# First mixer of a two-layer decoder step: GELU and swish as one ScalarE instruction each, layer norm as two VectorE operations

## The chip, the cores and the metric

The kernel runs on one core of one Trainium2 chip. The metric is the device time of one execution in microseconds (us), and the median of the runs stands for a kernel. The engines are named as the profile names them: PE is TensorE (its matmuls; PEld is its weight load), DVE is VectorE, ACT is ScalarE, POOL is GpSimd, and SP is SyncE, whose queue issues the weight transfers.

## The reference, cut to what matters

The step serves 256 prompt positions and 64 sample positions (NT = 320 columns in all) with the same weights. The first layer has the mixer that the change touches; `u`, `v` and `gate` are three of the six column blocks of one input projection.

```python
def layer_norm(x, g, b):
    mu = jnp.mean(xf, axis=-1, keepdims=True)
    xc = xf - mu
    y = xc * lax.rsqrt(jnp.mean(xc * xc, axis=-1, keepdims=True) + EPS)
    return y * g + b

def sgu_mix(u, v, ln_g, ln_b, w_s, b_s):
    vn = layer_norm(v, ln_g, ln_b)
    ...
    mixed = jnp.einsum('gts,bnsgd->bntgd', w, vc) + b_s[...]
    return u * mixed.reshape(b, l, SGU_WIDTH), vc

def even_mixer(h, pos, s0, w_in, ln_g, ln_b, w_s, b_s, w_out):
    z = h @ w_in
    u, v, q, k, vr, gate = jnp.split(z, EVEN_SPLITS, axis=-1)
    a_out, v_rows = sgu_mix(jax.nn.gelu(u), jax.nn.gelu(v), ln_g, ln_b, w_s, b_s)
    ...
    b_out = o * jax.nn.silu(gate)
    y = jnp.concatenate([a_out, b_out], axis=-1) @ w_out
```

`jax.nn.gelu` is the tanh form. Behind the mixer come a cross attention and an MLP, then a second layer with windowed attention, a cross attention and an MLP; none of that is changed.

## The kernel before, in words

Every weight is split in two parts, `whi` (written by ACT as a rounding copy of the staged weight) and `wlo` (DVE: staged weight minus `whi`), and every projection is three matmuls for each pair of a weight tile and an activation tile (`whi` with the rounded activations, `whi` with their rest, `wlo` with the rounded ones). A weight piece of 1 MB comes in through SP into one of three `stage` buffers; it is split into two halves of 128x1024, and the split of the next piece is made while PE works on this one (`weights`, `split`). So PE can begin a group of 48 matmuls only when ACT and DVE have made that group's halves, and SP can issue a load only when the piece three places earlier has been consumed.

Projections come in two shapes. `gemm2` makes two chunks of features (128x320 each) in two PSUM banks called `mm`; with `serial` the first chunk is finished before the second is begun. `gemm_tok` makes tokens on partitions (128x512) for two prompt blocks and a folded sample block. Each group has an `evac` that takes the banks out. Small matmuls of the retention and the spatial mix use four banks called `at`; they stand in the PE queue at fixed places, by `hook`.

The mixer runs in this order: q and k (four `gemm2` groups), v of the gMLP (two `gemm_tok` blocks of two weight pieces, evacuated into `VA`, with `bn_stats` on each tile), v of the retention (two blocks, `VR`) with `layer_norm` hooked into the first of their pieces, u (four groups, evacuated into `AHh`/`ALl`, which the profile calls HH and HL), the first half of the output projection with the retention states of the samples beside it (`ret_cross`, `ret_upd`, each state written back by the POOL queue as `o_ret_s`), the gates (four groups into `BH`/`BL`, again HH and HL in the profile), and the second half of the output projection.

The scheduler of the framework sets the order on each engine from the program and its own estimates; each engine then runs its queue strictly in order. All compute instructions are recorded by one wrapper (`InOrder.call`), so they share line 64 (62 in the changed kernel) and are told apart by the names of their tiles: `t` are the 128x320 work tiles of an evacuation, `w` the 128x512 ones, `k` and `k8b` tiles of the retention.

GELU of u is written here as z = u/2 (the row `nm.RB` was halved by POOL beforehand), ACT Square, a DVE operation, ACT Tanh, a POOL product of z with the mixed values, and a DVE operation `(p + 1) * z`. GELU of v is the same with a copy out of PSUM in front. The swish is ACT Tanh of half the gate, the POOL product with the retention output, and the same DVE operation. `layer_norm` takes mean and scale off with one DVE operation for each of three tiles (128x1024 twice, 64x1024) and applies gain and bias with two POOL operations for each.

Of the kernel before, what the change touches and what calls it, by code (L numbers as in the profile page):

```python
# [12 lines left out]
AF = mybir.ActivationFunctionType  # L13
ALU = mybir.AluOpType
# [3 lines left out]
P = 128  # L18
NT = 320
# [3 lines left out]
GC = 0.7978845608028654  # L23
GA = 0.044715
# [51 lines left out]
def decoder_step(ctx: ExitStack, tc: tile.TileContext, d, plan):  # L76
# [9 lines left out]
    def sb(shape, tag, bufs=1, dt=F32):  # L86
        cnt[0] += 1
        return pool.tile(list(shape), dt, tag=tag, bufs=bufs, name=f"{tag}_{cnt[0]}")
# [551 lines left out]
    A.activation(warm, ones[:, 0:1], AF.Exp)  # L640
# [58 lines left out]
    def rs_apply():  # L699
        for c in (4, 5, 6, 7, 0, 1, 2, 3):  # L700
            (V if c % 4 == 3 else G).tensor_tensor(QK[:, c], QK[:, c], nm.RB, op=ALU.mult)
        G.tensor_scalar(nm.RB, nm.RB, 0.5, 0.0, op0=ALU.mult, op1=ALU.add)
# [74 lines left out]
    for blk in range(2):  # L777
        def evac(ps, blk=blk):
            for tb in range(3):
                w = P if tb < 2 else 64  # L780
                z = sb([P, 512], "w2", W2)
                if tb < 2:
                    A.activation(z, ps[tb], AF.Copy, scale=nm.rs[:, tb:tb + 1])
                else:
                    fs = fold_sample(ps[2], 512, False)
                    V.tensor_scalar(z[:64], fs, nm.rs[:64, 2:3], None, op0=ALU.mult)
                p = sb([P, 512], "w2", W2)
                A.activation(p[:w], z[:w], AF.Square)
                V.scalar_tensor_tensor(p[:w], p[:w], 1.0 / GA, z[:w], op0=ALU.add, op1=ALU.mult)
                A.activation(p[:w], p[:w], AF.Tanh, scale=GC * GA)  # L790
                o = VA[tb][:, blk * 512:(blk + 1) * 512]
                V.scalar_tensor_tensor(o, p[:w], 1.0, z[:w], op0=ALU.add, op1=ALU.mult)
                V.bn_stats(stats[:w, tb, blk], o)
        gemm_tok([("w_in", "tok", 1024 + blk * 512, kh) for kh in range(2)], nm.h, nm.l, XS, 512, evac)
# [5 lines left out]
    def layer_norm():  # L800
        for tb in range(3):
            w = P if tb < 2 else 64
            V.bn_aggr(ag[:w, tb], stats[:w, tb])
        V.tensor_scalar(lt, ag[:, :, 1], 0.25, EPS, op0=ALU.mult, op1=ALU.add)
        rsqrt_into(lr, lt, [P, 3])
        V.tensor_scalar(lr, lr, 0.5, None, op0=ALU.mult)
        for tb in range(3):
            w = P if tb < 2 else 64
            vt = VA[tb]
            V.tensor_scalar(vt, vt, ag[:w, tb, 0:1], lr[:w, tb:tb + 1], op0=ALU.subtract, op1=ALU.mult)  # L810
            G.tensor_tensor(vt, vt, lngb[:w, 0], op=ALU.mult)
            G.tensor_tensor(vt, vt, lngb[:w, 1], op=ALU.add)
        G.dma_start(d["sgu_v"], VA[2])
# [160 lines left out]
    for g in range(4):  # L974
        def evac(ps, i0=0, g=g):
            for i in range(len(ps)):
# [3 lines left out]
                p = sb([P, NT], "t1", 3)  # L980
                A.activation(p, z, AF.Square)
                V.scalar_tensor_tensor(p, p, 0.25 / GA, z, op0=ALU.add, op1=ALU.mult)
                A.activation(p, p, AF.Tanh, scale=8.0 * GC * GA)
# [11 lines left out]
                G.tensor_tensor(z, z, mix, op=ALU.mult)  # L995
                V.scalar_tensor_tensor(z, p, 1.0, z, op0=ALU.add, op1=ALU.mult)
# [8 lines left out]
    for g in range(4):  # L1005
        def evac(ps, i0=0, g=g):
            for i in range(len(ps)):
# [3 lines left out]
                p = sb([P, NT], "t1", 3)  # L1011
                A.activation(p, z, AF.Tanh)
                G.tensor_tensor(z, z, ON[0][:, c], op=ALU.mult)
                V.scalar_tensor_tensor(z, p, 1.0, z, op0=ALU.add, op1=ALU.mult)
# [599 lines left out]
```

## Time and profile before

| what | value |
|---|---|
| median of 3 runs | 1123.97 us (1122.43 to 1125.91) |
| the profiled execution's own time | 1124.34 us |
| its span, first to last instruction | 1122.6 us |
| mean granted TensorE clock of the span | 0.989 |
| busy: PE, PEld, DVE, ACT, POOL | 1086.4, 1021.9, 738.8, 524.2, 136.3 us |
| chain that ended last, by engine | PE 74%, DVE 13%, DMA 5%, ACT 4%, issue 2%, POOL 1% |

The busy times are those of one profiled execution. A matmul's record reaches into that of the next, so that a busy PE may still be late; how far apart matmuls start tells more. In the chain of work that ended last, time put down to DVE, ACT, POOL or a transfer is time in which the path to the end ran through them; it isn't all a hole of PE, since that path also runs through work that PE had just caught up with.

### The profile page before, as it was taken

What the parts mean: (1) busy time and instruction counts of PE and PEld (TensorE: products, weight loads), DVE (VectorE), ACT (ScalarE), POOL (GpSimd) and SP (SyncE); (2) the same over time, 40 slices, a digit from 0 to 9 for tenths busy, and PEclk for the clock granted to TensorE, in tenths of its full rate; (3) what the DMA queues carried; (4) which work ended last, traced back from release to release, by engine and by line L of the source; (5) the groups of instructions that cost most, each with busy time, mean ns of one, the idle gap of its engine ahead of it and who ended that gap; (6) DMA issues with size and microseconds to landing.
All of it is one profiled execution on the core that took longest, in us unless ns stands there. A gap on an engine that the chain in (4) does not pass through costs nothing.

```text
span 1122.6 us, 18500 instructions
## 1 busy us (share of the span) xinstructions
PE 1086.4 (97%) x7424; PEld 1021.9 (91%) x7424; DVE 738.8 (66%) x1447; ACT 524.2 (47%) x910; POOL 136.3 (12%) x131
## 2 busy tenths in 40 slices
PE   7998999999999999999999989999999999999996
PEld 7886979999987999999999988879968999999995
DVE  8999885776545575555556898956536855555543
ACT  6454641545325355444445557745323654343432
POOL 4506030123000010000001222002000200000001
PEclk9999999999999999999999989999999999999998
DMA  9432337744787644444444334547576444444421
GB/s 349 146 128 98 131 119 271 287 148 152 296 328 309 263 151 150 151 150 151 150 151 150 121 113 156 188 149 278 209 300 264 149 150 151 150 151 150 151 75 48
DMA packets 30982, 201.55 MB, mean 180 GB/s; under 512 B 3624, under 2 KB 4792, under 8 KB 7992
## 3 DMA queue, kind: packets, MB, share of 16 engines
q1 hardware_dynamic: 27584, 187.13, 45.8%
q0 software_dynamic: 2512, 11.54, 2.8%
q10 hardware_dynamic: 800, 1.70, 0.5%
q8 instruction: 58, 0.95, 0.3%
q14 instruction: 28, 0.23, 0.1%
HBM read 187.51 MB, written 12.85 MB: 178 GB/s over the span
## 4 chain that ended last, share of the span: by engine, by line
PE 74%; DVE 13%; DMA 5%; ACT 4%; issue 2%; POOL 1%; SPq 0%; ACTq 0%; DVEq 0%; POOLq 0%
PE mm L64 64%; PE at L64 10%; DVE wlo L64 5%; DMA stage<-ws 4%; DVE t L64 2%; ACT whi L64 2%; DVE w L64 1%; POOL t L64 1%; DVE XL L64 1%; ACT w L64 1%; ACT k L64 1%; DVE Z L64 0%; DVE k8b L64 0%; DVE nw_u L64 0%; DVE X L64 0%
## 5 line engine op out<-in xcount | busy, mean ns | idle before, releaser
L64 DVE TENSOR_TENSOR wlo<-stage,whi 128x1024 fp32r<-128x1024 f32 (+1 forms) x270 | 339.5, 1264 | 191.6 <-ACT whi L64 189.9
L64 ACT ACTIVATE whi<-stage 128x1024 fp32r<-128x1024 f32 (+1 forms) x270 | 280.2, 1050 | 363.5 <-PE mm L64 273.4
L64 PE MATMUL mm<-HH,whi 128*128 128x320 f32 (+1 forms) x960 | 294.4, 308 | 2.2 <-ACT HH L64 2.2
L64 PE MATMUL mm<-HL,whi 128*128 128x320 f32 (+1 forms) x960 | 293.8, 306 | 0.3 <-DVE HL L64 0.2
L64 PE MATMUL mm<-HH,wlo 128*128 128x320 f32 (+1 forms) x960 | 293.3, 306 | 0.0
L64 PE MATMUL mm<-XH,whi 128*128 128x320 f32 x912 | 286.9, 315 | 5.3 <-ACT whi L64 5.3
L64 PE MATMUL mm<-XH,wlo 128*128 128x320 f32 x912 | 283.9, 311 | 5.5 <-DVE wlo L64 5.3
L64 PE MATMUL mm<-XL,whi 128*128 128x320 f32 x912 | 283.4, 311 | 0.0
L64 PEld LDWEIGHTS mm<-HH,whi 128*128 128x128 f32 x960 | 180.7, 188 | 4.9 <-ACT HH L64 2.4
L64 PEld LDWEIGHTS mm<-HL,whi 128*128 128x128 f32 x960 | 181.0, 189 | 1.0 <-DVE HL L64 0.8
L64 PEld LDWEIGHTS mm<-HH,wlo 128*128 128x128 f32 x960 | 180.9, 188 | 0.1
L64 PEld LDWEIGHTS mm<-XH,whi 128*128 128x128 f32 x912 | 172.8, 189 | 6.9 <-ACT whi L64 5.3
L64 PEld LDWEIGHTS mm<-XH,wlo 128*128 128x128 f32 x912 | 172.6, 189 | 6.7 <-DVE wlo L64 6.7
L64 PEld LDWEIGHTS mm<-XL,whi 128*128 128x128 f32 x912 | 172.8, 189 | 0.7
L64 POOL TENSOR_TENSOR ssq<-ssq,sqt 128x320 f32<-128x320 f32 x39 | 41.6, 1068 | 609.0 <-ACT sqt L64 608.1
L64 DVE TENSOR_TENSOR X<-mm,X 128x320 f32<-128x320 f32 x112 | 51.7, 488 | 56.8 <-PE mm L64 56.6
L64 ACT ACTIVATE t<-t 128x320 f32<-128x320 f32 x88 | 38.0, 462 | 24.1 <-DVE t L64 24.1
L64 DVE SCALAR_TENSOR_TENSOR t<-mm,RB 128x320 f32<-128x320 f32 x64 | 30.1, 491 | 25.5 <-PE mm L64 22.6
L64 ACT ACTIVATE HH<-t 128x320 fp32r<-128x320 f32 x80 | 34.5, 462 | 21.6 <-DVE t L64 21.1
L64 DVE TENSOR_TENSOR HL<-t,HH 128x320 fp32r<-128x320 f32 x80 | 37.0, 491 | 9.9 <-ACT HH L64 9.3
L64 DVE SCALAR_TENSOR_TENSOR XL<-X,cv,XH 128x320 fp32r<-128x320 f32 x48 | 38.4, 822 | 4.7 <-ACT XH L64 4.7
L64 ACT ACTIVATE XH<-X,cv 128x320 fp32r<-128x320 f32 x48 | 26.3, 554 | 21.1 <-DVE X L64 19.3
(240 smaller groups left out, 1139.3 us busy)
## 6 DMA issues: line engine op xcount, KB each, us to landing
stage<-ws SPq DMA_DIRECT2D x162, 1024.0 KB, 4.8
o_ret_s<-stage POOLq DMA_DIRECT2D x8, 512.0 KB, 6.9
HH<-ws SPq DMA_DIRECT2D x4, 1024.0 KB, 6.8
HL<-ws SPq DMA_DIRECT2D x4, 1024.0 KB, 6.6
k8a<-ws SPq DMA_DIRECT2D x2, 1024.0 KB, 8.3
o_mem_k<-k8a POOLq DMA_DIRECT2D x2, 1024.0 KB, 8.2
o_mem_v<-k8b POOLq DMA_DIRECT2D x2, 1024.0 KB, 10.6
cst<-ce SPq DMA_DIRECT2D x1, 1296.0 KB, 10.3
```

Source lines behind the costliest of these rows:

```text
L64: r = f(*a, **k)
```

## The change

GELU becomes one ACT instruction (`Gelu_apprx_tanh`), for v read from the PSUM bank with the row scale as the instruction's scale, for u in place on the scaled tile. Swish becomes one ACT instruction (`Silu`) in place. The products with the mixed values and with the retention output move from POOL to DVE, and take the place of the DVE operations that closed the old forms. Layer norm becomes two DVE operations for each tile: (v - mean) * gain, and then * rstd + bias; its six POOL operations are gone, and so is POOL's halving of `nm.RB`.

```diff
-    A.activation(warm, ones[:, 0:1], AF.Exp)
+    A.activation(warm, ones[:, 0:1], AF.Gelu_apprx_tanh)
...
             (V if c % 4 == 3 else G).tensor_tensor(QK[:, c], QK[:, c], nm.RB, op=ALU.mult)
-        G.tensor_scalar(nm.RB, nm.RB, 0.5, 0.0, op0=ALU.mult, op1=ALU.add)
...
         def evac(ps, blk=blk):
             for tb in range(3):
                 w = P if tb < 2 else 64
-                z = sb([P, 512], "w2", W2)
+                o = VA[tb][:, blk * 512:(blk + 1) * 512]
                 if tb < 2:
-                    A.activation(z, ps[tb], AF.Copy, scale=nm.rs[:, tb:tb + 1])
+                    A.activation(o, ps[tb], AF.Gelu_apprx_tanh, scale=nm.rs[:, tb:tb + 1])
                 else:
                     fs = fold_sample(ps[2], 512, False)
-                    V.tensor_scalar(z[:64], fs, nm.rs[:64, 2:3], None, op0=ALU.mult)
-                p = sb([P, 512], "w2", W2)
-                A.activation(p[:w], z[:w], AF.Square)
-                V.scalar_tensor_tensor(p[:w], p[:w], 1.0 / GA, z[:w], op0=ALU.add, op1=ALU.mult)
-                A.activation(p[:w], p[:w], AF.Tanh, scale=GC * GA)
-                o = VA[tb][:, blk * 512:(blk + 1) * 512]
-                V.scalar_tensor_tensor(o, p[:w], 1.0, z[:w], op0=ALU.add, op1=ALU.mult)
+                    A.activation(o, fs, AF.Gelu_apprx_tanh, scale=nm.rs[:64, 2:3])
                 V.bn_stats(stats[:w, tb, blk], o)
...
-        V.tensor_scalar(lt, ag[:, :, 1], 0.25, EPS, op0=ALU.mult, op1=ALU.add)
+        V.tensor_scalar(lt, ag[:, :, 1], EPS, None, op0=ALU.add)
         rsqrt_into(lr, lt, [P, 3])
-        V.tensor_scalar(lr, lr, 0.5, None, op0=ALU.mult)
         for tb in range(3):
...
-            V.tensor_scalar(vt, vt, ag[:w, tb, 0:1], lr[:w, tb:tb + 1], op0=ALU.subtract, op1=ALU.mult)
-            G.tensor_tensor(vt, vt, lngb[:w, 0], op=ALU.mult)
-            G.tensor_tensor(vt, vt, lngb[:w, 1], op=ALU.add)
+            V.scalar_tensor_tensor(vt, vt, ag[:w, tb, 0:1], lngb[:w, 0], op0=ALU.subtract, op1=ALU.mult)
+            V.scalar_tensor_tensor(vt, vt, lr[:w, tb:tb + 1], lngb[:w, 1], op0=ALU.mult, op1=ALU.add)
         G.dma_start(d["sgu_v"], VA[2])
...
                 V.tensor_tensor(z, ps[i][:, :NT], nm.RB, op=ALU.mult)
-                p = sb([P, NT], "t1", 3)
-                A.activation(p, z, AF.Square)
-                V.scalar_tensor_tensor(p, p, 0.25 / GA, z, op0=ALU.add, op1=ALU.mult)
-                A.activation(p, p, AF.Tanh, scale=8.0 * GC * GA)
+                A.activation(z, z, AF.Gelu_apprx_tanh)
                 mp = bank("at")
...
-                G.tensor_tensor(z, z, mix, op=ALU.mult)
-                V.scalar_tensor_tensor(z, p, 1.0, z, op0=ALU.add, op1=ALU.mult)
+                V.tensor_tensor(z, z, mix, op=ALU.mult)
                 A.activation(AHh[:, c], z, AF.Copy)
...
                 V.tensor_tensor(z, ps[i][:, :NT], nm.RB, op=ALU.mult)
-                p = sb([P, NT], "t1", 3)
-                A.activation(p, z, AF.Tanh)
-                G.tensor_tensor(z, z, ON[0][:, c], op=ALU.mult)
-                V.scalar_tensor_tensor(z, p, 1.0, z, op0=ALU.add, op1=ALU.mult)
+                A.activation(z, z, AF.Silu)
+                V.tensor_tensor(z, z, ON[0][:, c], op=ALU.mult)
                 A.activation(BH[:, c], z, AF.Copy)
```

The queues of PE and SP hold the same instructions in the same order as before. DVE has 20 instructions fewer (14 of the GELU of v, 8 of the GELU of u, one of the scale, and three more for the layer norm), ACT 18 fewer and two table loads more, POOL 23 fewer. Behind the mixer the only difference is one of these table loads.

The DVE queue around the layer norm, before: `HH_478` and `k8b_480` are the v tiles, `e_ag` and `e_lr` the mean and the scale, `wlo_920` and `wlo_924` the split of the second piece of the second VR block, and `e_t` begins a norm of the retention.

```order
L64 TENSOR_SCALAR e_lr_778<-e_lr_778 128x3
L64 TENSOR_SCALAR HH_478<-HH_478,e_ag_775,e_lr_778 128x1024 x2
L64 TENSOR_SCALAR k8b_480<-k8b_480,e_ag_775,e_lr_778 64x1024
L64 TENSOR_TENSOR w_154_911<-at_781,w_153_909 64x512
L64 TENSOR_TENSOR wlo_920<-stage_917,whi_919 128x1024
L64 TENSOR_SCALAR k8b_480<-w_154_911,rs_333 64x512
L64 TENSOR_TENSOR wlo_924<-stage_917,whi_923 128x1024
L64 TENSOR_SCALAR e_t_946<-e_ss_942 128x2
```

The same place now; `HH_119` is the tile that holds gain and bias.

```order
L62 BN_AGGR e_ag_738<-e_st_481 64x2
L62 SCALAR_TENSOR_TENSOR HH_478<-HH_478,e_ag_738,HH_119 128x1024
L62 TENSOR_SCALAR e_lt_740<-e_ag_738 128x3
L62 SCALAR_TENSOR_TENSOR k8b_480<-k8b_480,e_ag_738,HH_119 64x1024
L62 TENSOR_TENSOR wlo_804<-stage_801,whi_803 128x1024
L62 TENSOR_TENSOR wlo_808<-stage_801,whi_807 128x1024
```

and, after the small operations of the scale,

```order
L62 SCALAR_TENSOR_TENSOR HH_478<-HH_478,e_lr_741,HH_119 128x1024 x2
L62 SCALAR_TENSOR_TENSOR k8b_480<-k8b_480,e_lr_741,HH_119 64x1024
L62 TENSOR_TENSOR w_142_870<-at_744,w_141_868 64x512
L62 TENSOR_TENSOR wlo_879<-stage_876,whi_878 128x1024
L62 TENSOR_SCALAR k8b_480<-w_142_870,rs_333 64x512
L62 TENSOR_TENSOR wlo_883<-stage_876,whi_882 128x1024
L62 TENSOR_SCALAR e_t_905<-e_ss_901 128x2
```

Of the first pass, one tile stands earlier in the queue, and two in front of the split of the first piece of the second VR block (`wlo_804`, `wlo_808`). The second pass stands in front of the split of its second piece (`wlo_879`, `wlo_883`), where the one pass of before stood.

The POOL queue from the halving of `nm.RB` to the first evacuations of u, before:

```order
L64 TENSOR_SCALAR RB_428<-RB_428 128x320
L64 TENSOR_TENSOR HH_478<-HH_478,HH_119 128x1024 x4
L64 TENSOR_TENSOR k8b_480<-k8b_480,HH_119 64x1024 x2
L64 DMA o_sgu_v<-k8b_480 64x1024
L64 TENSOR_TENSOR t_204_1176<-t_204_1176,t_207_1186 128x320
L64 TENSOR_TENSOR t_208_1193<-t_208_1193,t_211_1203 128x320
L64 DMA o_ret_p<-cst_118 128x1024
```

and now, up to the next compute of POOL, which is far behind the mixer:

```order
L62 DMA o_sgu_v<-k8b_480 64x1024
L62 DMA o_ret_p<-cst_118 128x1024
L62 DMA o_ret_s<-stage_1393 128x1024 x2
L62 DMA o_ret_s<-stage_1527 128x1024 x2
L62 DMA o_ret_s<-stage_1625 128x1024 x2
```

All of POOL's work on the mixer's values is gone; what is left are the issues of transfers.

The ACT queue at the first gate group, now (`t_322` and `t_323` are its two chunks, `whi_1983` and `whi_2055` weight splits, `HH_1900` the rounded result):

```order
L62 ACTIVATE whi_1987<-stage_1981 128x1024
L62 ACT_TABLE_LOAD
L62 ACTIVATE t_322_1969<-t_322_1969 128x320
L62 ACTIVATE t_323_1975<-t_323_1975 128x320
L62 ACTIVATE HH_1900<-t_322_1969 128x320
L62 ACTIVATE whi_2055<-stage_2053 128x1024
L62 ACTIVATE HH_1900<-t_323_1975 128x320
```

The table load stands between a weight split and the first swish; the second one stands in front of the first Exp of the cross attention's softmax.

## Rows read from the trace of the kernel before

**Rows 1.** The chain of work that ended last: start us, us, what.

```profile
408.83 220.86 PE mm L64 x1506
```

**Rows 2.** Timeline of PE, first u group: start us, us, instruction, [idle before it <-releaser].

```profile
108.36 0.31 PE L64 MATMUL mm<-XL,whi 128*128 128x320 f32 x1
112.30 0.64 PE L64 MATMUL mm<-XH,wlo 128*128 128x320 f32 x1 [3.62 <-DVE wlo L64]
...
117.97 0.31 PE L64 MATMUL mm<-XH,wlo 128*128 128x320 f32 x1
```

**Rows 3.** One stretch: us, busy PE, PEld, DVE, ACT, POOL, PEclk, DMA share, GB/s.

```profile
114.00:116.00 2.00, 2.00 (x9) 2.00 (x9) 1.84 (x7) 0.98 (x2) 0.00 (x0) 0.50 0.64 205
```

**Rows 4.** Timeline of DVE, from the layer norm to the split of u's weights.

```profile
90.18 1.53 DVE L64 TENSOR_SCALAR HH<-HH,e_ag,e_lr 128x1024 f32<-128x1024 f32 x2
91.63 2.86 DVE L64 TENSOR_SCALAR k8b<-k8b,e_ag,e_lr 64x1024 f32<-64x1024 f32 x1
...
95.25 2.58 DVE L64 TENSOR_TENSOR wlo<-stage,whi 128x1024 fp32r<-128x1024 f32 x1
97.87 2.51 DVE L64 TENSOR_SCALAR k8b<-w,rs 64x512 f32<-64x512 f32 x1
100.41 3.27 DVE L64 TENSOR_TENSOR wlo<-stage,whi 128x1024 fp32r<-128x1024 f32 x1
103.60 2.35 DVE L64 TENSOR_SCALAR e_t<-e_ss 128x2 f32<-128x2 f32 x1
...
111.03 2.35 DVE L64 TENSOR_TENSOR wlo<-stage,whi 128x1024 fp32r<-128x1024 f32 x2
```

**Rows 5.** Timeline of POOL over the layer norm.

```profile
91.08 11.51 POOL L64 TENSOR_TENSOR HH<-HH,HH 128x1024 f32<-128x1024 f32 x4 [38.28 <-DVE HH L64]
102.55 5.85 POOL L64 TENSOR_TENSOR k8b<-k8b,HH 64x1024 f32<-64x1024 f32 x2
```

**Rows 6.** Timeline of ACT: the rounding of u's first weights.

```profile
96.59 2.01 ACT L64 ACTIVATE whi<-stage 128x1024 fp32r<-128x1024 f32 x2 [2.81 <-PE at L64]
```

**Rows 7.** Timeline of PE, later in u: small matmuls that waited.

```profile
153.94 0.65 PE L64 MATMUL at<-k8b 64*64 64x256 f32 x4 [0.52 <-DVE t L64]
...
156.65 0.78 PE L64 MATMUL at<-k8a,w 128*128 128x256 f32 x4 [1.06 <-ACT k L64]
...
160.93 0.51 PE L64 MATMUL at<-k8a,w 128*128 128x256 f32 x2 [0.56 <-DVE stage L64]
```

**Rows 8.** Waits of DVE from 124 to 170 us: total, times, longest.

```profile
DVE t L64 <- POOL t L64: 4.0, 6, 0.8
```

**Rows 9.** Timeline of PE, second half of the output projection, first group.

```profile
233.85 0.31 PE L64 MATMUL mm<-HH,wlo 128*128 128x320 f32 x1
236.34 0.41 PE L64 MATMUL mm<-HH,whi 128*128 128x320 f32 x1 [2.17 <-ACT HH L64]
...
240.71 0.31 PE L64 MATMUL mm<-HL,whi 128*128 128x320 f32 x1
```

**Rows 10.** Timeline of DVE, the last gate chunk: its bank, its closing product.

```profile
232.93 0.48 DVE L64 TENSOR_TENSOR t<-mm,RB 128x320 f32<-128x320 f32 x1
...
235.29 0.49 DVE L64 SCALAR_TENSOR_TENSOR t<-t,t 128x320 f32<-128x320 f32 x1 [0.75 <-POOL t L64]
```

**Rows 11.** Timeline of POOL, the same chunk.

```profile
234.06 1.20 POOL L64 TENSOR_TENSOR t<-t,k 128x320 f32<-128x320 f32 x1 [3.11 <-ACT t L64]
```

**Rows 12.** Timeline of ACT: the table load, the first Tanh of a gate, the first Exp.

```profile
1.27 1.28 ACT L64 ACT_TABLE_LOAD   x1 [1.27 <-PEq L1582]
...
210.23 0.87 ACT L64 ACTIVATE t<-t 128x320 f32<-128x320 f32 x2 [0.74 <-DVE t L64]
...
306.93 0.47 ACT L64 ACTIVATE k<-at,sm_mx 128x256 f32<-128x256 f32 x1 [3.54 <-DVE sm_mx L64]
```

**Rows 13.** The chain again: the longest transfer of the mixer in it.

```profile
167.19 9.70 DMA stage<-ws
```

**Rows 14.** Waits of SP from 0 to 260 us: total, times, longest.

```profile
SPq L128 <- DMA o_ret_s<-stage: 25.6, 4, 11.2
```

More of the change, by code (lines that the diff above doesn't have):

```diff
@@ L22 @@
 EPS = 1e-6
-GC = 0.7978845608028654
-GA = 0.044715
 NEG = -1.0e30
```

## The prediction, made before the changed kernel ran

> **What bounds the kernel now.** PE does. I read the chain of work first: in its longest piece, the MLP of the first layer, 1506 matmuls stand in 220.86 us [rows 1], 0.1467 us from one start to the next. That is the pace of a 128x320 matmul that waits for nothing, and a group of 48 takes 7.04 us. Then I read PE's timeline over the mixer (the first 245 us) for places where starts lie further apart. Of two of them the size can be read off at once.
>
> Hole 1 is in the first u group. Its 2nd matmul starts at 108.36 and its 24th at 117.97 [rows 2]: 9.61 us for 22 steps, which at the pace take 3.23, so 6.4 us are lost. The hole itself is 3.94 - 0.15 = 3.8 us; it ends when DVE has made `wlo`. The other 2.6 us come behind it: the granted clock is 0.50 [rows 3], the lower level of 1.2 GHz, and PE goes at half pace although it has work.
>
> Hole 2 is in the second half of the output projection: from 233.85 to 240.71 there are 17 steps, worth 2.49 us [rows 9], so 4.4 us are lost, 2.3 in the hole, for ACT's HH, and the rest behind it at about half pace again.
>
> In between, the small matmuls of the retention wait three times, 0.52, 1.06 and 0.56 us [rows 7], 2.1 in all. Hole 1 loses about 0.2 more than the idle time that its row shows (3.8 against 3.62); with 0.2 for each of the three I count 2.7.
>
> The rest of the time, about 1110 us, is PE's own work and holes that the change doesn't reach.
>
> **The layer norm and hole 1.** Before u's first `wlo` at 111.03, DVE is slow at everything [rows 4]. A split takes 2.58 and 3.27 us, while the two at 111.03 take 2.35 together, 1.18 each. A 64x512 operation takes 2.51, though 128x1024 of the same kind took 0.76 (1.53 for two). An operation on two elements per lane takes 2.35. POOL works on the layer norm from 91.08 to 108.40 without a stop [rows 5], and the slow rows lie in exactly that stretch. Over 1.18, 0.7 and 0.2, these four rows waste 1.4 + 2.1 + 1.8 + 2.1 = 7.4 us.
>
> The change takes all of POOL's work there away and puts six operations on DVE where there were three. No row shows the fused form on 128x1024. The nearest is the split, also 128x1024 with two inputs from SBUF: 1.18. The bounds are 0.76, the old one-input form, and 2.35, twice the split. At 1.18 the six cost 7.1 us in place of 1.53 + 2.86 = 4.4, so 2.7 more. DVE reaches u's `wlo` 7.4 - 2.7 = 4.7 us earlier, at 106.3, and has it at 107.5. PE wants it with its third matmul, at 108.5, and the second half 24 matmuls after the group began, at 111.7, when it has been there since 108.7. ACT's part was ready at 98.6 [rows 6]. So the hole closes even by this narrow count, which leaves out DVE's reserve: the GELU of v loses 14 DVE instructions before the layer norm, each on half a split's columns, so some 0.6 us, 8 us in all (an estimate from the split). At 2.35 each the six would cost 7.0 more, which that reserve covers. I take the whole 6.4; the other end is 0, if POOL is not the cause. With no hole there is no slow clock behind it.
>
> The first pass of two tiles now stands ahead of the split of the second VR block's first piece. It adds at most 3 x 1.18 = 3.5 us there, and the 8 us cover it. If that cover failed, PE would wait there instead (rival 2). The transfer of `sgu_v` and the write-backs no longer stand behind POOL's products, which costs nothing.
>
> **GELU of u and the small waits.** From 124 to 170 us DVE stood waiting for POOL six times, 4.0 us in all [rows 8]: the product of z and the mixed values had to be done on POOL before DVE could close the chunk or reuse the one `t2` buffer. PE's small matmuls wait behind that for DVE to empty an `at` bank, or for ACT, whose copies stand behind HH. Now the product is DVE's own, in place of the closing operation (0.49 us, as that one [rows 10]), and another such operation per chunk is gone; ACT has one instruction per chunk less. The gain is between 0 and 2.7; since each of the three waits is under the time DVE gets back, I take 2.7. A transfer or PE itself is late next there.
>
> **The swish and hole 2.** For the last gate chunk DVE takes the bank at 232.93, POOL multiplies from 234.06 to 235.26 [rows 11], DVE closes until 235.78 [rows 10], ACT rounds, and PE goes on at 236.34. Now one DVE product of about 0.49 follows the swish: 1.2 us less, the lower bound. But the chunk is also late from the start. PE wants it 42 matmuls into its group, so the group began 6.2 us before 234.0, at 227.8; the bank was full then, and DVE took it 5.1 us later. Without POOL, a gate group's round over DVE and ACT is two scalings 0.96, a split 1.18, a product 0.49, two HH 0.87 (as the two Tanhs of [rows 12], which have their size), a rounding 1.0 [rows 6] and a split 1.18: 5.7 us against PE's 7.04. Each of the three groups ahead of the last makes up some 1.3 us, 4 in all. With the 1.2 that is over twice the hole of 2.3, so I take all of the 4.4.
>
> **The table loads.** Two are added. The load at the program's start took 1.28 us [rows 12]. The first new one stands before the first swish, where ACT had 0.74 us idle: 0.5 us late, which the gates' 1.3 us per group makes up. The second stands before the first Exp, behind 3.54 us of idle time. I count them at 0; on the path they would cost at most 2.6. The Trainium skill speaks against this change here: its page "ScalarE: Activation LUTs", section "What ACT_TABLE_LOAD costs", puts a switch of sets at about 2.66 us with the drain, twice the row. By it the sum would lose nothing if both stay covered, and 5.3 us if neither is.
>
> The new functions have no row. Tanh takes 0.44 us for 128x320, and I take the same. Below that is no gain. Above it a gate group leaves ACT 7.04 - 2.0 - 0.87 - 0.87 = 3.3 us free, so a swish of up to 2.1 us would still be hidden.
>
> **The sum.** 6.4 + 2.7 + 4.4 = 13.5 us. Against the profiled execution's own 1124.34 that gives 1110.8; it stands 0.37 above the median of the runs, so the median should be 1110.5. PE and SP keep their orders, and behind the mixer nothing else moves, so the gain is carried to the end.
>
> **Rivals.**
>
> 1. Transfers set the pace from 166 us on. The chain runs through a load of 9.70 us there [rows 13], and others follow it. If they don't start earlier, the 9.1 us gained ahead of them are lost and hole 2's 4.4 remain: 1119.6. For it: PE's lead over these loads is thin. Against: SP waited 25.6 us for the write-backs of the states [rows 14], and these follow DVE and PE, so they come earlier together. Chance 0.10.
> 2. The layer norm's first pass delays the VR split in front of which it stands. A hole of 2 us with 2.6 of slow clock behind it, as in hole 1: 1115.1. Against: the 8 us. Chance 0.10.
> 3. The table loads aren't covered: 1110.5 + 2.6 = 1113.1. By the page's figure it would be 1115.8. Against: the idle times of rows 12. Chance 0.08.
> 4. Slower than before: GELU and swish are much dearer than Tanh on ACT. Up to 2.1 us each is hidden; above it, u's and the gates' 16 instructions lengthen the path. It decides at 2.1 + 13.5/16 = 2.9 us, over six times Tanh; at 4 us the time is 1110.5 + 16 x 1.9 = 1141. Nothing that ACT does in these rows comes near that price. Chance 0.03.
> 5. It doesn't do what it says: POOL isn't what slows DVE. Then hole 1 stays and grows by the 2.7 of layer norm: 1123.97 - 7.1 + 2.7 = 1119.6. An operation on two elements per lane that takes 2.35 us can hardly be anything but waiting. Chance 0.05.
>
> **How the numbers follow.** The forecast keeps 0.64. Its own time can be 4 us better (waits of under half a microsecond that I didn't count, the runs' scatter) or, with only the lower bound of 1.2 for hole 2 and nothing in the middle, 5.9 worse. So the range is 1106.5 to 1117.5; it takes in rivals 2 and 3 and leaves out 0.18. About 0.3%, 3.4 us, is what a measurement of this kernel can tell from no change. Rivals 1 and 5 lie at its edge and I split them: 0.09 for no difference, 0.03 for slower, 0.88 for faster.
>
> **What would show it.** In the new profile, POOL computes nothing between 50 and 220 us; splits between 90 and 108 us take 1.2 us; PE's starts in the first u group keep 0.147 and the granted clock there is 1.00; the last gate chunk is ready before PE wants it. A PE wait for `wlo` near 85 us would be rival 2, one for `whi` behind a load after 160 us rival 1. The prediction is wrong if holes 1 and 2 close and the time doesn't fall by about 11 us, for then something behind the mixer sets the end.

## The result, and the profile after

| | kernel before | changed kernel |
|---|---|---|
| median | 1124.72 us of 4 runs | 1108.26 us of 4 runs (1107.71 to 1110.15) |
| the profiled execution's own time, span | 1124.34, 1122.6 us | 1110.15, 1108.0 us |
| mean granted TensorE clock | 0.989 | 0.995 |

The ratio is 0.9857, with a 95% interval of 0.9842 to 0.9872: 16.5 us faster by the medians, 14.2 by the two profiled executions. The forecast was 1110.5, its range 1106.5 to 1117.5. A second measurement of the changed kernel, beside the last experiments, gave 1108.22.

The page of the changed kernel: busy time of each engine, and the chain of work that ended last, by engine.

```profile
PE 1079.5 (97%) x7424; PEld 1018.4 (92%) x7424; DVE 716.3 (65%) x1427; ACT 519.3 (47%) x894; POOL 98.8 (9%) x108
...
PE 88%; DVE 6%; ACT 2%; DMA 2%; issue 1%; SPq 0%; ACTq 0%; DVEq 0%
```

POOL lost 37.5 us of work and DVE 22.5, and PE's share of the chain rose from 74 to 88%: fewer pieces of the path run through anything but matmuls. PE's waits from 0 to 245 us (total, times, longest) are those of the program's start and 1.3 us for `wlo`, all before 60 us; both big holes are gone. The signs that the prediction named came: POOL computes nothing from 50 to 220 us, splits take 1.2, the granted clock in the first u group is 1.00.

```profile
PE mm L62 <- ACT whi L62: 5.8, 1, 5.8
PE mm L62 <- DVE wlo L62: 1.3, 3, 0.5
```

**Hole 1.** Timeline of DVE, in place of rows 4:

```profile
80.32 1.22 DVE L62 SCALAR_TENSOR_TENSOR HH<-HH,e_ag,HH 128x1024 f32<-128x1024 f32 x1
82.74 2.35 DVE L62 TENSOR_TENSOR wlo<-stage,whi 128x1024 fp32r<-128x1024 f32 x2
...
87.17 2.48 DVE L62 SCALAR_TENSOR_TENSOR HH<-HH,e_lr,HH 128x1024 f32<-128x1024 f32 x2
...
91.60 1.23 DVE L62 TENSOR_TENSOR wlo<-stage,whi 128x1024 fp32r<-128x1024 f32 x1
92.86 0.49 DVE L62 TENSOR_SCALAR k8b<-w,rs 64x512 f32<-64x512 f32 x1
93.37 1.22 DVE L62 TENSOR_TENSOR wlo<-stage,whi 128x1024 fp32r<-128x1024 f32 x1
94.52 0.16 DVE L62 TENSOR_SCALAR e_t<-e_ss 128x2 f32<-128x2 f32 x1
...
97.67 2.35 DVE L62 TENSOR_TENSOR wlo<-stage,whi 128x1024 fp32r<-128x1024 f32 x2
```

The four slow operations of rows 4 are here again, at 1.23, 0.49, 1.22 and 0.16 us: 3.1 in place of 10.7. A fused operation takes 1.24. u's first `wlo` is ready at 98.9; PE takes it at 107.61, 8.7 us later, and goes on at its pace:

```profile
107.32 0.30 PE L62 MATMUL mm<-XH,whi 128*128 128x320 f32 x1
107.46 0.31 PE L62 MATMUL mm<-XL,whi 128*128 128x320 f32 x1
107.61 0.31 PE L62 MATMUL mm<-XH,wlo 128*128 128x320 f32 x1
107.75 0.31 PE L62 MATMUL mm<-XH,whi 128*128 128x320 f32 x1
```

**Hole 2.** The last gate chunk goes ACT, DVE, ACT now (`t<-t` on ACT is the swish, `t<-t,k` the product, in place of rows 10 and 11):

```profile
217.45 0.47 ACT L62 ACTIVATE t<-t 128x320 f32<-128x320 f32 x1 [0.39 <-DVE t L62]
...
218.41 0.48 DVE L62 TENSOR_TENSOR t<-t,k 128x320 f32<-128x320 f32 x1
...
218.92 0.47 ACT L62 ACTIVATE HH<-t 128x320 fp32r<-128x320 f32 x1 [1.00 <-DVE t L62]
```

The chunk is rounded at 219.4; PE wants it at 222.1 and doesn't wait.

**The table loads** (in place of rows 12) still take 1.28 each; no wait of PE stands behind either.

```profile
198.01 1.28 ACT L62 ACT_TABLE_LOAD   x1
199.31 0.83 ACT L62 ACTIVATE t<-t 128x320 f32<-128x320 f32 x2
...
290.65 1.28 ACT L62 ACT_TABLE_LOAD   x1 [3.32 <-DVE sm_mx L62]
```

**Where the time came from.** PE runs the same matmuls in the same order in both kernels, so the start of the same matmul can be laid side by side. The 553rd, behind the first u group, starts at 120.86 us before and 113.58 after: a lead of 7.28. The 481st has 0.42, so the first u group gave 6.86. In this way, for the changed kernel and for every experiment below (lead over the kernel before, us, in its profiled execution; good to about 0.02):

| kernel | to 100 us | first u group | u and the states, to the gates | gates, end of projection | to 386 us | behind | sum |
|---|---|---|---|---|---|---|---|
| changed | 0.43 | 6.86 | 4.61 | 4.36 | -1.54 | -0.08 | 14.64 |
| after_again (the same) | 0.78 | 6.85 | 4.62 | 4.37 | 0.47 | -0.12 | 16.97 |
| ln_alone | 0.63 | 6.86 | 2.13 | 0.15 | -1.89 | -0.41 | 7.47 |
| ln_on_pool | 0.77 | 6.23 | 4.62 | 4.35 | 0.47 | -0.46 | 15.98 |
| pool_beside | -8.70 | 6.66 | 4.61 | 4.37 | 0.47 | -0.24 | 7.17 |
| u_mix_on_pool | 0.81 | 6.85 | 4.62 | 4.36 | 0.48 | 0.19 | 17.31 |
| u_old | 1.02 | 6.85 | 1.67 | 4.36 | -1.88 | 0.30 | 12.32 |
| gate_on_pool | 0.33 | 6.85 | 4.62 | 3.91 | 0.47 | -0.27 | 15.91 |
| close_on_dve | 0.60 | 6.86 | 4.28 | 1.92 | 0.48 | -0.33 | 13.81 |
| gate_old | 0.17 | 6.85 | 4.63 | 0.06 | 0.20 | 0.23 | 12.14 |
| more_tables | -0.74 | 6.86 | 4.61 | -1.99 | -2.66 | -0.06 | 6.02 |
| qk_off_pool | 1.88 | 6.85 | 4.62 | 3.73 | -1.41 | 0.62 | 16.29 |
| all_off_pool | 2.18 | 6.86 | 4.62 | 4.37 | 0.47 | 5.84 | 24.34 |

(In more_tables, all_off_pool and, by one pair, qk_off_pool a few matmuls changed places.) The forecast had 6.4, 2.7 and 4.4 for the second to fourth column. The changed kernel's profile gives 1.54 back before 386 us, in a hole in the cross attention, in the chain of a weight load that landed late:

```profile
367.45 1.13 PE L62 MATMUL at<-cst,k8b 128*128 128x256 f32 x4 [1.76 <-DVE HL L62]
```

The same kernel measured again has no such hole and 0.47 gained there. So it belongs to single executions and not to the change (the profiles of ln_alone, u_old, more_tables and qk_off_pool have it too); the profiled execution, with it, is the longest of its four.

### The profile page after: what moved, and what is told of

Same layout as the page of the kernel before. It is cut to its first block, busy times and chain, and to the rows that moved or that the text cites. A ratio compares the mean times of both kernels' runs of the same rounds, so it can differ in the third digit from the quotient of the medians.

```text
span 1108.0 us, 18438 instructions
## 1 busy us (share of the span) xinstructions
PE 1079.5 (97%) x7424; PEld 1018.4 (92%) x7424; DVE 716.3 (65%) x1427; ACT 519.3 (47%) x894; POOL 98.8 (9%) x108
## 4 chain that ended last, share of the span: by engine, by line
PE 88%; DVE 6%; ACT 2%; DMA 2%; issue 1%; SPq 0%; ACTq 0%; DVEq 0%
PE mm L62 75%; PE at L62 13%; DVE wlo L62 2%; DMA stage<-ws 1%; DVE XL L62 1%; DVE t L62 1%; DVE w L62 1%; ACT whi L62 1%; DVE Z L62 0%; DVE X L62 0%; ACT XH L62 0%; DMA X<-x 0%; ACT w L62 0%; ACT Z L62 0%; ACT sqt L62 0%
## 5 line engine op out<-in xcount | busy, mean ns | idle before, releaser
L62 DVE TENSOR_TENSOR wlo<-stage,whi 128x1024 fp32r<-128x1024 f32 (+1 forms) x270 | 334.3, 1245 | 198.1 <-ACT whi L62 196.4
L62 ACT ACTIVATE t<-t 128x320 f32<-128x320 f32 x80 | 34.0, 460 | 17.9 <-DVE t L62 17.9
L62 ACT ACTIVATE HH<-t 128x320 fp32r<-128x320 f32 x80 | 34.5, 462 | 11.2 <-DVE t L62 10.7
```

The lines of the kernel that those rows point to most:

```text
L62: r = f(*a, **k)
```

## The experiments

**Is it GpSimd that slows VectorE, or what waits for it?** pool_beside leaves every order of the changed kernel alone and only gives GpSimd work that nobody waits for (six products of which nothing is used):

```diff
         G.dma_start(d["sgu_v"], VA[2])
+        for i in range(6):
+            h = P if i < 4 else 64
+            G.tensor_tensor(lngb[:h, 0], lngb[:h, 0], lngb[:h, 1], op=ALU.mult)
```

> The changed kernel with six products added on GpSimd, of the layer norm's old shapes (four 128x1024, two 64x1024), on a tile that nobody needs any more and whose result nobody reads. No order on any other engine changes; only the write-back of sgu_v stands behind them on GpSimd. They run from about 83 to 100 us. Theory: VectorE's operations in that stretch lengthen although nothing waits for GpSimd's results: splits 1.2 to 2.5 us or more; about 7 to 10 us are lost on VectorE, u's first wlo comes at 106 to 109 where PE wants it at 105, and hole 1 is back: 2 to 6 us longer than the changed kernel. Rival 5: VectorE's rows keep their lengths, 0 us.

1119.09 us (ratio to the kernel before 0.9950, 0.9934 to 0.9967): 10.8 longer than the changed kernel, where 2 to 6 were expected. Timelines of POOL and DVE:

```profile
81.79 4.48 POOL L62 TENSOR_TENSOR HH<-HH 128x1024 f32<-128x1024 f32 x1 [33.42 <-DVE k8b L62]
86.35 2.41 POOL L62 TENSOR_TENSOR HH<-HH 128x1024 f32<-128x1024 f32 x1
...
81.64 2.34 DVE L62 TENSOR_TENSOR wlo<-stage,whi 128x1024 fp32r<-128x1024 f32 x2
83.91 2.38 DVE L62 TENSOR_SCALAR nw_u<-e_lt 128x3 int32<-128x3 int32 x1
86.32 0.17 DVE L62 TENSOR_SCALAR e_lr<-nw_u 128x3 int32<-128x3 int32 x1
86.52 2.25 DVE L62 TENSOR_TENSOR nw_u<-e_lr 128x3 f32<-128x3 f32 x1
88.81 0.16 DVE L62 SCALAR_TENSOR_TENSOR nw_u<-nw_u,e_lt 128x3 f32<-128x3 f32 x1
89.01 2.23 DVE L62 SCALAR_TENSOR_TENSOR e_lr<-nw_u,e_lr 128x3 f32<-128x3 f32 x1
```

A product takes 2.4 us; only the first takes 4.48, and it stands beside two splits that keep their undisturbed length (2.34 for both). Behind them every second of DVE's operations on three elements per lane takes 2.2 to 2.4 in place of 0.16, six of them up to 98.63: DVE stands still for most of a product, gets two operations in, and stands for the next. This is contention and not a dependency: nothing in the program joins the two. The page "SBUF — State Buffer" of the Trainium skill, section "SBUF: two separate sides", has GpSimd and VectorE (for its operations with two inputs from SBUF or in a two-port mode) share a pair of ports as an exclusive lock that whoever starts first holds for the whole instruction. By that rule a small operation pays the rest of a long one, and so does a product that starts behind a split; the trace agrees (2.2 to 2.4 us and 4.48).

The loss was mis-sized because what stood beside GpSimd were eleven small operations, and not the splits that the expectation had lengthened: a small one lost 2.0 to 2.2 us, as much as a split loses in rows 4 (1.4 and 2.1). And the hole didn't come back at u but some 12 us ahead of it, before the last weights of the retention's v, where PE waited 7.7 us for a split (PE's waits, 60 to 245 us):

```profile
PE mm L62 <- DVE wlo L62: 7.7, 1, 7.7
```

**The layer norm alone,** and the rest without it. ln_alone is the kernel before with the two fused operations:

```diff
-            V.tensor_scalar(vt, vt, ag[:w, tb, 0:1], lr[:w, tb:tb + 1], op0=ALU.subtract, op1=ALU.mult)
-            G.tensor_tensor(vt, vt, lngb[:w, 0], op=ALU.mult)
-            G.tensor_tensor(vt, vt, lngb[:w, 1], op=ALU.add)
+            V.scalar_tensor_tensor(vt, vt, ag[:w, tb, 0:1], lngb[:w, 0], op0=ALU.subtract, op1=ALU.mult)
+            V.scalar_tensor_tensor(vt, vt, lr[:w, tb:tb + 1], lngb[:w, 1], op0=ALU.mult, op1=ALU.add)
```

> The kernel before with one part of the change: layer norm as two VectorE operations for each tile and nothing of it on GpSimd. GELU and swish stay as they were. The first hole's price by itself. From the mean (about 87.6 us) to u's first wlo the new order has some 15.8 us of VectorE work at undisturbed lengths (two passes of 3.8 us, splits 1.2 each, small operations 0.2 each), so that wlo comes at about 103.4 and PE wants it at 108.5: hole 1 and the slow clock behind it are gone without the help of the shorter GELU of v, 6.4 us less than the kernel before, about 1118. Rival (the shorter GELU of v is needed too): part of the hole stays, 0 to 3 us less. Hole 2 and the waits from 124 to 170 us stay as they were in either case.

1115.79 us (0.9920, 0.9904 to 0.9936): 8.9 less than before. The first u group gained 6.86, exactly as in the full change, and u behind it 2.13 more. DVE makes u's two `wlo` at 99.64 and 100.85, earlier than the 103.4 expected:

```profile
99.64 1.21 DVE L64 TENSOR_TENSOR wlo<-stage,whi 128x1024 fp32r<-128x1024 f32 x1
100.85 1.21 DVE L64 TENSOR_TENSOR wlo<-stage,whi 128x1024 fp32r<-128x1024 f32 x1
```

In the kernel before, one slow operation more than rows 4 show stood in front of them:

```profile
106.19 2.24 DVE L64 TENSOR_SCALAR e_r<-nw_u 128x2 int32<-128x2 int32 x1
```

And from 110 to 175 us ln_alone's VectorE waits for GpSimd as long as in rows 8, although u gained:

```profile
DVE t L64 <- POOL t L64: 4.1, 6, 0.8
```

ln_on_pool is the opposite, the changed kernel with these lines the other way round.

> The changed kernel with the layer norm as it was: one VectorE operation for each tile, then gain and bias on GpSimd (six products). GELU and swish stay one instruction each. Theory (GpSimd's work slows VectorE): between about 82 and 100 us, while GpSimd works, weight splits take 2.5 to 3.3 us in place of 1.2, and small operations up to 2.3. From the layer norm's start to u's first wlo it was 22 us before; it now starts about 7 us earlier than before since the GELU of v is shorter, so u's wlo comes at about 104.7 and PE wants it at about 105: a hole of 0 to 2 us with some slow clock behind it, 0 to 4 us longer than the changed kernel. Rival 5 (GpSimd isn't what slows VectorE): splits stay at 1.2 us, VectorE has three operations fewer, and the time is the changed kernel's within 1 us.

1111.42 us (0.9876, 0.9856 to 0.9896), 3.2 longer by the medians. VectorE's rows are slow again, 4.56 for two splits where 2.35 is undisturbed, but no hole is left in the profile, since the layer norm begins at 81.56 where it was 90.18 [rows 4]:

```profile
82.51 6.62 POOL L62 TENSOR_TENSOR HH<-HH,HH 128x1024 f32<-128x1024 f32 x2 [33.36 <-ACT whi L62]
...
82.29 4.56 DVE L62 TENSOR_TENSOR wlo<-stage,whi 128x1024 fp32r<-128x1024 f32 x2
...
86.78 2.91 DVE L62 TENSOR_SCALAR HH<-HH,e_ag,e_lr 128x1024 f32<-128x1024 f32 x1
...
95.24 2.26 DVE L62 TENSOR_SCALAR e_t<-e_ss 128x2 f32<-128x2 f32 x1
...
104.74 2.35 DVE L62 TENSOR_TENSOR wlo<-stage,whi 128x1024 fp32r<-128x1024 f32 x2
```

u's first `wlo` is ready at 106.0 and PE takes it at 107.26, only 1.3 us later. So the layer norm off GpSimd closes hole 1 by itself, and the shorter GELU of v in front of it did so in this execution, by a thin margin. The profile is of ln_on_pool's shortest run (1108.91, the others 1110.95 to 1112.39); it loses only 0.6 in the first u group, and where the others lose their 2 to 3 us more was not seen.

**The products of u and of the gates.** Each alone back on GpSimd, with nothing behind it; first u's, in u_mix_on_pool:

```diff
-                V.tensor_tensor(z, z, mix, op=ALU.mult)
+                G.tensor_tensor(z, z, mix, op=ALU.mult)
```

> The changed kernel with one edit: the product of GELU(u) with the mixed values goes back to GpSimd, eight times; no closing operation behind it. Theory (the round over GpSimd is what made the small matmuls of the retention late): waits of VectorE for GpSimd of 2 to 4 us in all return between 115 and 165 us, and the time is 2 to 4 us longer than the changed kernel. Rival (the shorter VectorE and ScalarE work gave this gain, not the product's engine): within 1 us of the changed kernel.

1107.68 us (0.9850, 0.9831 to 0.9869), no longer than the changed kernel. VectorE's waits did come, by way of ScalarE: from 110 to 175 us it stands 7.2 us for HH (1.1 in the changed kernel), whose rounding now stands behind GpSimd; PE waits for none of it. In gate_on_pool the other product goes back in the same way.

> The changed kernel with one edit: the product of the swish with the retention output goes back to GpSimd, eight times; no closing operation behind it. Theory (the product of 1.2 us on GpSimd in each round and in the last chunk's path made hole 2): a hole of PE in front of the last gate chunk returns, 0.5 to 2 us with slow clock behind it, 1 to 4.4 us longer. Rival (the closing operation and VectorE's load made it): no hole, within 1 us of the changed kernel.

1109.46 us (0.9862, 0.9844 to 0.9880), 1.2 longer; 0.45 of it at the gates, where PE shows no wait over 0.2. VectorE stands for HH here too (185 to 235 us, 0.5 in the changed kernel):

```profile
DVE HL L62 <- ACT HH L62: 7.5, 7, 2.1
```

In both the theory missed: which engine makes the product is worth next to nothing here. VectorE has eight operations fewer and stands longer, and PE's lead covers the difference. What is still missing from the old form is the operation on VectorE that waits for GpSimd. close_on_dve puts it back for both:

```diff
+                G.tensor_tensor(z, z, mix, op=ALU.mult)
+                V.scalar_tensor_tensor(z, z, 0.0, z, op0=ALU.add, op1=ALU.max)
...
+                G.tensor_tensor(z, z, ON[0][:, c], op=ALU.mult)
+                V.scalar_tensor_tensor(z, z, 0.0, z, op0=ALU.add, op1=ALU.max)
```

> The changed kernel with both products (u's and the gates') back on GpSimd and, behind each, a VectorE operation in the place and shape of the old closing operation that changes no value (z + 0, larger of it and z). GELU and swish stay one ScalarE instruction each. Each product alone on GpSimd cost -0.6 and 1.2 us. Theory A (the loss was in VectorE standing in its queue for GpSimd in front of the closing operation): VectorE's waits for GpSimd come back, about 4 us from 115 to 165 us and 4 us in the gates, the small matmuls of u lose 2 to 4 us and hole 2 comes back with 1.5 to 4.4: 4 to 8 us longer than the changed kernel. Rival B (Square, the operation behind it and Tanh made the round long): 1 to 2 us longer, as with the gates' product alone.

1112.23 us (0.9887, 0.9867 to 0.9907), 4.0 longer. VectorE's waits from 110 to 175 us, then from 185 to 240, then PE's from 110 to 245:

```profile
DVE t L62 <- POOL t L62: 4.6, 6, 0.8
```
```profile
DVE t L62 <- POOL t L62: 4.6, 5, 1.6
```
```profile
PE mm L62 <- ACT HH L62: 1.8, 1, 1.8
```

VectorE stands 4.6 us for GpSimd in both places, but PE pays in the gates alone: 2.44 there (1.92 against 4.36), 0.33 in u. (The profile is of the shortest of its four runs, so that part of the 4.0 isn't in it.) Product and closing operation together bring hole 2 back, as theory A has it for the gates; for u it fails. Standing alone doesn't explain the gates, though, for gate_on_pool stood longer. VectorE takes the last gate chunk's bank at 219.24 there and at 220.80 here (216.87 in the changed kernel):

```profile
219.24 0.48 DVE L62 TENSOR_TENSOR t<-mm,RB 128x320 f32<-128x320 f32 x1
```
```profile
220.80 0.48 DVE L62 TENSOR_TENSOR t<-mm,RB 128x320 f32<-128x320 f32 x1
```

With the eight closing operations back in its queue VectorE is 1.6 us later, and the last of them, 0.49 us, stands in the chunk's own path. How much of the 2.44 is the standing and how much these operations' own time was not separated.

**The old forms whole.** u_old is the changed kernel with u's GELU as before, gate_old with the swish as before.

```diff
+                p = sb([P, NT], "t1", 3)
+                A.activation(p, z, AF.Square)
+                V.scalar_tensor_tensor(p, p, 0.25 / GA, z, op0=ALU.add, op1=ALU.mult)
+                A.activation(p, p, AF.Tanh, scale=8.0 * GC * GA)
...
+                G.tensor_tensor(z, z, mix, op=ALU.mult)
+                V.scalar_tensor_tensor(z, p, 1.0, z, op0=ALU.add, op1=ALU.mult)
```

> The changed kernel with u's GELU written out as before: Square, a VectorE operation, Tanh, the product on GpSimd, the closing operation on VectorE. Layer norm, GELU of v and the swish stay changed. With only the last two of these five (close_on_dve) VectorE waited 4.6 us for GpSimd in u and PE lost nothing; with the layer norm alone changed PE still lost 0.9 us near 150 us and 1.4 near 170 against the changed kernel. Theory C (the two ScalarE and one VectorE operations that are gone gave these): PE's losses of 0.9 and 1.4 come back, 1.5 to 3 us longer than the changed kernel. Rival D (the lead from the layer norm and the GELU of v covers u as well): under 1 us.

1111.72 us (0.9886, 0.9868 to 0.9904), 3.5 longer. PE loses 2.94 in u (1.67 against 4.61), in waits like those of rows 7:

```profile
150.88 0.51 PE L64 MATMUL at<-k8a,w 128*128 128x256 f32 x2 [0.56 <-DVE stage L64]
```

Theory C holds: it takes Square, the VectorE operation and Tanh to lose this time; product and closing operation alone didn't. No run has the three without the product on GpSimd, so whether they would do it by themselves is open.

> The changed kernel with the swish written out as before: Tanh, the product on GpSimd, the closing operation on VectorE; no table load for the swish then. GELU and layer norm stay changed. With product and closing operation back (close_on_dve) a hole of 2.1 us stood in front of the last gate chunk at full clock behind it, 2.45 us lost; the kernel before lost 4.4 there, its hole 2.4 and half clock behind. Theory (the round over GpSimd is the whole of hole 2, and the clock decides between the two sizes): a hole of 2.0 to 2.5 us, and 2.4 us longer with the clock at 1.00, 4.2 to 4.4 with 0.50 behind the hole. Rival (Silu's own form gave part of it): a hole clearly over 2.5 us.

1112.87 us (0.9899, 0.9876 to 0.9922), 4.6 longer; the gates lose 4.30, the whole of what the change had gained. PE's hole, and the clock behind it (columns as in rows 3):

```profile
224.61 0.42 PE L62 MATMUL mm<-HH,whi 128*128 128x320 f32 x1 [2.11 <-ACT HH L62]
```
```profile
226.00:228.00 2.00, 2.00 (x9) 2.00 (x9) 2.00 (x4) 1.82 (x3) 0.00 (x0) 0.50 0.48 201
```

and the same two of close_on_dve:

```profile
224.21 0.41 PE L62 MATMUL mm<-HH,whi 128*128 128x320 f32 x1 [1.80 <-ACT HH L62]
```
```profile
226.00:228.00 2.00, 2.00 (x16) 2.00 (x15) 2.00 (x4) 1.89 (x4) 0.00 (x0) 1.00 0.25 102
```

A hole 0.31 us longer, and PE got 9 matmuls into these two microseconds in place of 16. Of the 4.30, 2.44 come with the product and the closing operation, and most of the remaining 1.86 is the clock.

**What a table costs.** more_tables puts an Exp of one element (of no use) ahead of each swish:

```diff
+                A.activation(sb([P, 1], "warm"), z[:, 0:1], AF.Exp)
                 A.activation(z, z, AF.Silu)
```

> The changed kernel with a one-element Exp in front of each of the gates' eight swishes, its result unused, so that ScalarE changes its table twice for each chunk: some 16 loads more where there was one. The order of PE changes slightly in the gates and the output projection behind them. By the load's row (1.28 us) four loads and two Exps make 5.5 us per gate group where ScalarE has 3.3 us free: the first loads are hidden and about 2.2 us per group are not, 5 to 10 us in all longer than the changed kernel. If a switch costs 2.66 us as the Trainium skill, page "ScalarE: Activation LUTs", section "What ACT_TABLE_LOAD costs", has it with the drain: some 11 us per group and 25 to 32 us longer. Rival (loads run beside the other work and are hidden): under 2 us.

1116.59 us (0.9926, 0.9907 to 0.9945), 8.3 longer: within what 1.28 a load gives and far from what 2.66 would. The gates lose 6.4 in the profile, but not by 2.2 in each group: ACT has no idle time left there, PE waits once, 3.6 us for `whi` at 213.9, and the granted clock is 0.50 behind that. ACT's timeline:

```profile
203.20 0.20 ACT L62 ACTIVATE warm<-t 128x1 f32<-128x1 f32 x1
203.31 0.45 ACT L62 ACTIVATE HH<-t 128x320 fp32r<-128x320 f32 x1
203.78 1.28 ACT L62 ACT_TABLE_LOAD   x1
205.07 0.47 ACT L62 ACTIVATE t<-t 128x320 f32<-128x320 f32 x1
```

A load starts 0.02 us behind the operation ahead of it, and the next begins 0.01 behind the load. The 2.66 us per switch of the page "ScalarE: Activation LUTs" of the Trainium skill, section "What ACT_TABLE_LOAD costs", contain a drain that these rows don't show; the measurement decides.

**The same step elsewhere.** qk_off_pool moves GpSimd's fifteen products in q and k to VectorE:

```diff
-            (V if c % 4 == 3 else G).tensor_tensor(QK[:, c], QK[:, c], nm.RB, op=ALU.mult)
+            V.tensor_tensor(QK[:, c], QK[:, c], nm.RB, op=ALU.mult)
...
-                    G.tensor_tensor(sw, sw, cec("sin"), op=ALU.mult)
+                    V.tensor_tensor(sw, sw, cec("sin"), op=ALU.mult)
...
-        G.tensor_tensor(qxi, Qf[:, :, P:2 * P], qxi, op=ALU.mult)
+        V.tensor_tensor(qxi, Qf[:, :, P:2 * P], qxi, op=ALU.mult)
```

> The changed kernel with the same step taken in q and k (10 to 50 us): the eight products with the sine table, the six with the rstd row and one with the decay row go from GpSimd to VectorE, so that GpSimd computes nothing from about 10 us to the end of the mixer's projections. It costs VectorE 15 operations of about 0.49 us, 7.6 us. Theory: VectorE's other rows there are lengthened by GpSimd now (two small products into Z 0.28 each when alone, 3.94 for six between 41 and 45 us; splits 1.9 to 3.0 where 1.2 is undisturbed), they give back 7 us or more, and the holes at 46.7 and 50.1 us (0.81 and 0.65) close: 0 to 2 us faster than the changed kernel. Rival: VectorE is full there and 7.6 us more make it the bound: a few us slower.

1108.06 us (0.9846, 0.9826 to 0.9866): not to be told from the changed kernel by the median. In the profile six small products into Z take 0.69 us where the expectation read 3.94, and PE has 1.45 us more lead at 100 us than in the changed kernel, part of which is the scatter of the first transfers; the two small holes that the expectation named are gone. all_off_pool adds the ten operations of the second layer's rotation:

```diff
-            G.tensor_tensor(QA[:, 2 * g], p, q, op=ALU.subtract)
+            V.tensor_tensor(QA[:, 2 * g], p, q, op=ALU.subtract)
...
-            G.tensor_tensor(QA[:, 2 * g + 1], p, q, op=ALU.add)
+            V.tensor_tensor(QA[:, 2 * g + 1], p, q, op=ALU.add)
```

> The changed kernel with GpSimd's products in q and k (fifteen) and in the second layer's windowed attention (ten: sums and differences of the rotation of q) on VectorE. There PE waits 3.8 us at 653 us for VectorE to write Z, whose splits take 1.9 in place of 1.2 us beside GpSimd. The order of PE around 640 to 700 us changes with it (the products with Z stand later). Theory: splits there go back to 1.2 us, the hole of 4.1 us shrinks by 2 us or more, and with 0 to 1 us from q and k: 2 to 4 us faster than the changed kernel. Rival: the ten operations of 0.49 us cost VectorE what the splits give back, and the hole stays: within 1 us of the changed kernel.

1100.17 us (0.9790, 0.9769 to 0.9811), 8.1 faster than the changed kernel, better than both. Against the second measurement of the changed kernel, the table has 6.0 of it behind 386 us and 1.4 before 100. Groups of DVE from 620 to 700 us (busy, mean ns of one), of this kernel and then of the changed one:

```profile
L62 DVE TENSOR_TENSOR wlo<-stage,whi 128x1024 fp32r<-128x1024 f32 x19 | 23.1, 1216 | 0.9 <-ACT whi L62 0.9
...
L62 DVE TENSOR_TENSOR k<-t,t 128x320 f32<-128x320 f32 x10 | 4.8, 481 | 0.0
```
```profile
L62 DVE TENSOR_TENSOR wlo<-stage,whi 128x1024 fp32r<-128x1024 f32 x16 | 25.0, 1568 | 0.5 <-ACT whi L62 0.4
```

A split costs 0.35 us less, so the 4.8 us that VectorE took over are paid back by some fourteen splits. PE's wait of 3.8 us for Z is gone. But the order of PE changed there too: how much of the gain is the engine and how much the order was not separated.

## Why the prediction was right, point by point

- **Hole 1, 6.4 us.** Right in size (6.86, of which 0.5 is a small hole at 103.7 that was not counted) and in cause: pool_beside shows the contention by itself, and ln_alone the whole gain from the layer norm alone. The margins were mis-sized. The narrow count let the layer norm bring u's `wlo` 4.7 us earlier; in ln_alone it begins at 99.64 in place of 111.03, 11.4 earlier. The step that missed is the list of slow operations: it left out a fifth, at 106.19, which makes 6.7. The other 4.7 lie with DVE's new order, in which the small operations of the two norms alternate and u's splits stand ahead of the last of them; that is read from the timelines and not tested. Nor was DVE "slow at everything": between the slow rows one operation took 0.70 (at 94.52) and one 0.17 (at 105.99). The reserve of 8 us was right in itself: with the shorter GELU of v alone the layer norm begins 8.6 us earlier (ln_on_pool). But the two don't add up: in the changed kernel `wlo` begins at 97.67, 2.0 ahead of ln_alone. That it came 8.7 ahead of PE, where the narrow count and the reserve make 9.0, is luck.
- **The price of a fused operation.** 1.18 was taken from the split, 1.24 was measured: the nearest row was a good one.
- **The small waits, 2.7 us.** Right for the three waits that were counted (2.8), too small for the stretch, and put down to the wrong cause. 4.6 us came, since two holes outside rows 7 (at 131.8 and 181.1, 0.4 and 1.3) went with them. The step that failed is "PE's small matmuls wait behind that": VectorE's waits for POOL of rows 8 were true, but with them back in close_on_dve PE lost only 0.33, and in ln_alone, where they stand as before, PE gained 2.13 all the same, by the lead that the layer norm gave. Undoing u's GELU lost 2.9, with Square, the VectorE operation and Tanh back beside the POOL product.
- **Hole 2, 4.4 us.** Right in size (4.36) and in the round over GpSimd as its cause, but not by the 1.2 us of the product's place, the "lower bound": the product alone on GpSimd costs 0.45. With the closing operation that waits for it, and with the next bank's scaling behind that, it costs 2.44, and the clock most of the rest.
- **Table loads at 0, the functions like Tanh.** Right: the first load had no idle time in front of it at all and was still hidden; `Silu` and `Gelu_apprx_tanh` both take 0.45 to 0.48 for 128x320, as the Tanhs did. That ACT has about 3.3 us free per gate group is borne out in kind by more_tables, where 5.5 us per group left ACT no idle time; the loss there was one hole with a slow clock behind it, so it doesn't measure the 3.3.
- **The rivals.** Transfers (rival 1) didn't set the pace: the lead of 11.9 us at 170 us was kept and 4.36 added, although SP's wait for the states' write-backs is still there (25.4 us, rows 14 had 25.6). Rivals 2 to 5 didn't come. pool_beside shows rival 2's place, though: delayed from 84 us on, DVE was late for the split of the retention's v first.
- **The sum.** 13.5 against 14.2 in the profiled execution and 16.5 by the medians. Of the 2.3 between these two, 1.9 is that the profiled execution, with its late load, is that much above its kernel's median, and 0.4 that the one before is below its own. What the sum lacks are mainly the holes outside rows 7 and at 103.7. The range's upper end, 1117.5, doesn't follow from its sentence either: 5.9 above the forecast is 1116.4.

## What to carry to other kernels

Look on VectorE for short operations that take as long as GpSimd's long ones; where they stood in this kernel, GpSimd's elementwise work cost VectorE more than doing it there did. An engine's wait in its queue is a loss only where somebody has run out of lead behind it: undo the wait alone before putting a hole down to it. A product could stay on the slow engine here: it took work off the busy one while it made that one wait, and the lead covered the rest. An operation of the busy engine behind it used the lead up, at least in the gates.

## What the runs showed of the chip that was not expected

An operation on 128x3 takes 2.2 to 2.4 us beside GpSimd's products of 2.4 us and loses as much as one on 128x1024, so that a run of small operations was the worst place for GpSimd to work. GpSimd pays too: its first product in pool_beside took 4.48 us beside two splits.

And two holes of PE at the same place, 1.80 and 2.11 us of idle time, had granted clocks of 1.00 and 0.50 (1.2 GHz) behind them. With 16 matmuls in 220 to 222 us ahead of both, 0.31 us more of hole cost about 1.9 us more, 4.3 in place of 2.4. Idle time alone doesn't decide it: 2.02 us in the gates of ln_alone had 0.50 behind them, 2.08 us in the cross attention of u_old 1.00.
